# Value blocks in pairs of 512 columns, pass-one tiles and tables in the second weight slot, block 2's rounding copies behind the last h

## The chip, the cores and the metric

One core of a Trainium2 chip. The metric is the device time of one execution in microseconds (us). The kernel before took 1279.45 us, the median of three runs (1277.96 to 1279.61).

## What is computed

One layer of a bidirectional encoder trunk, for one sequence of 2048 tokens of 1024 float32 values. Cut to what matters here:

```python
mod = c_act @ w_ada + b_ada; shift, scale, gate = split(mod, 3)
h = rmsnorm(x, norm_w) * (1 + scale) + shift                  # 2048 x 1024
proj = h @ w_in + b_in                                        # 1024 x 4624
na_q, na_k, na_v, na_z, ml_q, ml_k, ml_v, ml_o, ml_z, gates = split(proj)
na_out = neighbourhood_attention(na_q, na_k, na_v, rpb) * silu(na_z)
mq, mk = split(silu(short_conv(concat(ml_q, ml_k))), 2)
hm = mlstm(mq, mk, ml_v, gates) + flip(mlstm(flip(...)))      # 4 heads of 128, chunks of 64 tokens
ml_out = norm(hm * sigmoid(ml_o)) * ml_norm_w * silu(ml_z)
y = concat(na_out, ml_out) @ w_out;  out = rmsnorm(x + gate * y, final_norm_w)
```

The change is in the input projection `h @ w_in`, above all in the columns ml_v and ml_o (packed by head: a block holds v and o of one head) and na_v, and in places that later stages borrow.

## The kernel before, in words

**Products.** Every float32 operand of a large product is split in a high and a low part, and a product is three matmuls for each of KT = 8 slices of 128 of the contraction (mm3, L636): high by high, high by low, low by high. h lies with its channels on the partitions, as hhi and hlo, in NG = 4 groups of 512 tokens (GT); a group has four token tiles of 128.

**Blocks.** The columns of w_in come in blocks of 256. Blocks 0 to 3 are v and o of the four mLSTM heads (vo_group, L700), block 0 with 16 gate columns more; 4 and 5 are na_v (nav_group, L667). Their result has tokens on the partitions: one token tile is 24 matmuls of 256 columns into one PSUM buffer of the pool `pp` (four buffers), which DVE evicts with one addition of the bias row `brow` (L711, L674). A group of vo gets a sigmoid on ACT (L717) and goes to memory (`d_ck`). Blocks 6 to 9 are computed the other way round, 512 tokens per matmul (`pc`, conv_blocks). Later stages compute the rest (`pq`, L1094) between steps of the mLSTM, where they are pumped in as cover.

**Weights.** There are two slots, `whi_a`/`wlo_a` and `whi_b`/`wlo_b`, used in turn. raw_w (L197) loads a block in two halves of four slices, each half into its one buffer `raw0` or `raw1`; ACT copies it, rounded, into the high part (L207), and DVE subtracts for the low part (L208). SP issues the loads in program order, and each issue waits for whatever it needs: the buffer, and the transfer that stood eight earlier on its lane (names DMAHW0 to DMAHW7).

**The start** (start, L213 to L573) is written out by hand. It computes mod on DVE, h of group 0 slice by slice (first_h, L404: two ACT passes, `hhi` and `h`; DVE makes hlo, L405) and the products of blocks 0 and 1 with each slice k (products, L436). Block 2's group 0 (a third weight place, `w_extra`, borrowed from a later h) follows; its halves are rounded on ACT by high_w2 (L445) at k = 5 and 6, ahead of that slice's products and behind its h, and subtracted on DVE by low_w2 (L449). Then come groups 1 to 3 of blocks 0 and 1, with h of the next group made in between.

**The token blocks** (tok_blocks, L776): block 2's groups 1 to 3, then blocks 3, 4 and 5, each with all four groups, one slot after the other. While a block runs, the next one's halves are loaded at its beginning and split after its groups 1 and 2. One step of a chain of small work is taken after every eviction: gate rows and their two transposes on TensorE (L813), absolute value, exponential and logarithm (L827, L828), scans, decays, gate sums (`gsum`, with loads `ga`), and the column sums `ps_cols` on TensorE (L877). SP also issues nine fills of attention tables (`d_t`, L759) and the preparation of their bias (`d_e`, `rneg`).

**Later places.** Pass one of the mLSTM (ml_pass1) reads tiles `kv` (seven buffers) and weighs them for the two directions. Pass two writes its result in place into `zt` (end, L1405), from which it is stored to `d_mix`. The attention stage keeps four tables `tab` and a ring of ten buffers, four of which are the places of hm and zt.

## Time and profile before

| | |
|---|---|
| median of three runs | 1279.45 us |
| profiled execution | 1278.1 us |
| its span | 1276.3 us |
| granted TensorE clock, mean | 0.997 of full speed |
| TensorE (PE) busy | 1265.2 us, 99% of the span |
| VectorE (DVE) busy | 791.9 us, 62% |
| ScalarE (ACT) busy | 539.3 us, 42% |
| GpSimd (POOL) busy | 201.4 us, 16% |

The span is the time from the first to the last instruction of the profiled execution. A group's "mean ns" is the length of one instruction; matmuls overlap, so what one of them costs is read from the distance of two starts. In a row of the timeline stand its start, its length, the engine, the line, the operation and, in square brackets, how long the engine had been idle before it and what ended that. PEclk in a window is the clock that TensorE was granted, as a share of full speed.

### The profile page before, as it was taken

To read this page: it belongs to the slowest core of one execution; us is meant where nothing else is said; L and a number is where in the kernel's file an instruction comes from. 1 tells how busy PE (TensorE), PEld (TensorE's weight loads), DVE (VectorE), ACT (ScalarE), POOL (GpSimd) and SP (SyncE) were. 2 spreads that over 40 slices of the span, in tenths; PEclk is the share of its full clock that TensorE was granted. 3 is DMA by queue.
4 is the path that set the end of the run, shared out by engine and by line. 5 is a ranking of instruction groups with operands and counts; after the bars stand their busy time and mean duration, and the time that the engine had idled before them with its cause. 6 is when DMAs were issued, how large, how long until landed. Compare 5 with 4: busy or idle time off the path is not lost.

```text
span 1276.3 us, 22945 instructions
## 1 busy us (share of the span) xinstructions
PE 1265.2 (99%) x8168; PEld 1096.9 (86%) x8168; DVE 791.9 (62%) x2391; ACT 539.3 (42%) x1183; POOL 201.4 (16%) x368
## 2 busy tenths in 40 slices
PE   9999999999999999999999999999999999999997
PEld 8999999999888888888888888888877888888886
DVE  7766542213667665266777878877557766767664
ACT  6652425442333222123333324323357565565552
POOL 0000003341000000000001001001324431332541
PEclk9999999999999999999999999999999999999999
DMA  9999937987678754745757867746678755655551
GB/s 366 333 308 281 305 123 200 238 228 199 188 173 200 167 147 109 212 126 168 201 170 204 243 195 218 233 156 180 208 251 265 229 163 161 203 176 178 173 175 67
DMA packets 217082, 259.08 MB, mean 203 GB/s; under 512 B 23435, under 2 KB 163595, under 8 KB 216968
## 3 DMA queue, kind: packets, MB, share of 16 engines
q1 hardware_dynamic: 149542, 190.09, 51.7%
q0 software_dynamic: 13616, 37.28, 9.0%
q10 hardware_dynamic: 53810, 30.24, 8.4%
q8 instruction: 65, 1.06, 0.3%
q14 instruction: 49, 0.40, 0.1%
HBM read 173.05 MB, written 92.72 MB: 208 GB/s over the span
## 4 chain that ended last, share of the span: by engine, by line
PE 94%; DMA 4%; DVE 1%; issue 1%; ACT 0%; SPq 0%; POOL 0%; ACTq 0%; POOLq 0%
PE pq L1094 27%; PE y L1676 14%; PE pc L640 5%; PE pc L641 5%; PE pc L639 5%; PE pO L1633 4%; PE pT L1618 3%; PE pvo L639 3%; PE pvo L641 3%; PE pvo L640 3%; PE pS L1587 3%; PE pvo L694 3%; PE pv L641 2%; PE pv L640 2%; PE pv L639 2%; PE pi L1346 2%
## 5 line engine op out<-in xcount | busy, mean ns | idle before, releaser
L1094 PE MATMUL pq<-hhi,whi_a 128*128 128x512 f32 x512 | 208.4, 407 | 0.0
L1094 PE MATMUL pq<-hlo,whi_a 128*128 128x512 f32 x512 | 207.9, 406 | 0.0
L1094 PE MATMUL pq<-hhi,wlo_a 128*128 128x512 f32 x512 | 207.2, 405 | 0.0
L1368 POOL TENSOR_TENSOR hm<-hm,ck 128x128 f32<-128x128 f32 x64 | 28.3, 442 | 576.3 <-DVE hm L1367 541.5
L1094 PEld LDWEIGHTS pq<-hhi,wlo_a 128*128 128x128 f32 x512 | 96.8, 189 | 16.6 <-issue 0.2
L1094 PEld LDWEIGHTS pq<-hlo,whi_a 128*128 128x128 f32 x512 | 96.8, 189 | 16.1 <-issue 0.4
L1094 PEld LDWEIGHTS pq<-hhi,whi_a 128*128 128x128 f32 x512 | 96.8, 189 | 16.0
L1599 ACT ACTIVATE ring<-ring,mn 128x480 f32<-128x480 f32 (+5 forms) x128 | 75.9, 594 | 55.8 <-DVE mn L1598 55.8
L1620 ACT ACTIVATE ring<-pT 96x384 f32<-96x384 f32 (+3 forms) x128 | 65.8, 514 | 63.3 <-PE pT L1618 61.8
L1676 PE MATMUL y<-hhi,wlo_a 128*128 128x512 f32 (+1 forms) x272 | 87.0, 394 | 0.2 <-ACT y L1683 0.2
L1676 PE MATMUL y<-hhi,whi_a 128*128 128x512 f32 x256 | 86.3, 408 | 0.0
L1349 ACT ACTIVATE num<-px,gtile 128x129 f32<-128x129 f32 x120 | 38.7, 367 | 105.4 <-PE px L1344 91.7
L1522 POOL DMA_DIRECT2D v<-d_vna x158 | 79.1, 507 | 15.2 <-DMA xr<-in_x_p_dram 4.5
L1618 PEld LDWEIGHTS pT<-ident,ring 128*128 128x128 f32 (+2 forms) x416 | 51.0, 136 | 19.1 <-ACT ring L1620 3.8
L1618 PE MATMUL pT<-ident,ring 128*128 128x128 f32 (+2 forms) x416 | 66.2, 272 | 0.0
L639 PE MATMUL pvo<-whi_b,hhi 128*128 128x256 f32 x224 | 63.7, 284 | 0.0
L1598 DVE CUSTOM_DVE_ANT_0 ring<-pS,tab 128x480 f32<-128x480 f32 (+5 forms) x128 | 62.1, 540 | 2.6 <-PE pS L1587 2.3
L641 PE MATMUL pvo<-whi_b,hlo 128*128 128x256 f32 x224 | 63.2, 282 | 0.0
L640 PE MATMUL pvo<-wlo_b,hhi 128*128 128x256 f32 x224 | 63.0, 281 | 0.0
L934 ACT ACTIVATE dec<-dec,gtile 128x128 f32<-128x128 f32 x128 | 41.4, 391 | 50.6 <-POOL dec L927 45.9
L711 DVE TENSOR_TENSOR stvo<-pvo,brow 128x256 f32<-128x256 f32 x60 | 24.9, 421 | 53.2 <-PE pvo L641 41.3
L674 DVE TENSOR_TENSOR stv<-pv,brow 128x256 f32<-128x256 f32 x32 | 13.5, 425 | 71.5 <-PE pv L641 65.5
(357 smaller groups left out, 3338.3 us busy)
## 6 DMA issues: line engine op xcount, KB each, us to landing
ck<-d_ck SPq DMA_DIRECT2D x64, 384.5 KB, 3.5
rawq<-in_w_main_dram SPq DMA_DIRECT2D x28, 512.0 KB, 5.1
raw<-in_w_main_dram SPq DMA_DIRECT2D x18, 512.0 KB, 6.2
kv<-d_ck SPq DMA_DIRECT2D x64, 128.5 KB, 3.2
dec<-d_mneg SPq DMA_DIRECT2D x32, 256.0 KB, 6.4
d_ck<-dec ACTq DMA_DIRECT2D x32, 256.0 KB, 7.8
qs<-d_qna SPq DMA_DIRECT2D x30, 256.0 KB, 3.9
xr<-in_x_p_dram POOLq DMA_DIRECT2D x15, 512.0 KB, 4.0
```

The lines of the kernel that those rows point to most:

```text
L639: nc.tensor.matmul(ps, lhi(k), rhi(k), start=(k == 0), stop=False)
L640: nc.tensor.matmul(ps, lhi(k), rlo(k), start=False, stop=False)
L641: self.mark = nc.tensor.matmul(ps, llo(k), rhi(k), start=False, stop=(k == KT - 1))
L934: nc.scalar.activation(t[:, o, :], t[:, o, :], AF.Exp, bias=self.cols["g"][:, d, h, c : c + 1])
L1094: self.mark = nc.tensor.matmul(patch_ps(ps) if patch else ps, w, self.htok(h, g, k, patch), start=(k == 0 and n == 0), stop=(k == KT - 1 a ...
L1522: queue.dma_start(chunks[key][r * nkc : (r + 1) * nkc, :], rows[r])
L1598: nc.vector.tensor_tensor_reduce(pt[:, :nk], ps, tabs[ct][:, j * nk : (j + 1) * nk], 1.0, 3e38, ALU.add, ALU.min, mn)
L1599: nc.scalar.activation(pt[:, :nk], pt[:, :nk], AF.Exp, bias=mn, scale=-1.0, accum_out=sums[:, j : j + 1])
L1618: nc.tensor.transpose(ps[:cs, i, :], U[u][j][:, i * cs : (i + 1) * cs], self.ident)
L1620: nc.scalar.activation(t[:cs, :nch, :], ps[:cs, :nch, :], AF.Copy)
L1633: nc.tensor.matmul(po[j * HD : (j + 1) * HD, ct, :], v[:n, h * HD : (h + 1) * HD], pt[j][:n, i, :], start=(i == 0), stop=(i == nch - 1))
L1676: nc.tensor.matmul(y, m[:, k, :], w[k][:, cs], start=(k == 4 and n == 0), stop=(k == 3 and n == 2))
```

## The change

- The two weight slots become one tile per part with a leading index of two (`wpair`), so that slots 0 and 1 lie side by side; both stay for the whole program.
- tok_blocks runs (block, group) in the order (2,1), (3,0), 2 and 3 together for groups 2 and 3, (3,1), (4,0), 4 and 5 together for groups 1 to 3, (5,0). "Together" is pair_group: one matmul of 512 columns reads 256 columns of either slot, and DVE evicts the two halves with one addition each. There are two more staging buffers.
- The halves of block 3 are loaded as soon as block 2's are split, at the end of the start (next_w), and split during (2,1); block 4's during (3,1), block 5's during (4,0), block 6's during (5,0).
- In the start, high_w2 moves from k = 5 and 6 to k = 6 and 7.
- The two gate transposes write one PSUM tile, one behind the other.
- Pass one's tiles lie in slot 1's high part and zt in its low part; both directions' weighted tiles are new tiles (eight buffers); end writes to hm, from which it is stored. Tables lie in slot 1 (the last of the first four loaded behind close); the ring has two places of hm and eight of its own.

The core of the diff:

```diff
-        for nm, pl in (("a", wa), ("b", wb)):
-            self.wslot.append(tuple(pl.tile([P, KT, 272 if nm == "a" else 256], F32R, name=f"w{part}_{nm}") for part in ("hi", "lo")))
+        self.wpair = tuple(wa.tile([P, 2, KT, 272], F32R, name=f"w{part}") for part in ("hi", "lo"))
+        self.wslot = [tuple(part[:, j] for part in self.wpair) for j in range(2)]
...
-            if k in (KT - 3, KT - 2):
-                high_w2(k - KT + 3)
-            if k == KT - 2:
-                low_w2(0)
+            if k in (KT - 2, KT - 1):
+                high_w2(k - KT + 2)
             if k == KT - 1:
                 for tt in range(4, 8):
                     square(tt, ssqs[1])
+                low_w2(0)
                 low()
                 low_w2(1)
...
         def next_w():
-            for part in self.raw_w(2, 0):
+            self.parts = []
+            for half, part in enumerate(self.raw_w(2, 0)):
                 yield
                 part(nc.vector)
+                self.parts.append(self.raw_part(3, 1, half))
...
+    def pair_group(self, blk, g):
...
+        for o in range(4):
+            ps = self.pp.tile([P, GT], F32, tag="pp", name=f"p2_{blk}_{g}_{o}")
+            self.mm3(
+                ps.rearrange("p (a c) -> p a c", a=2),
+                lambda k: self.hhi[g][:, k, o * P : (o + 1) * P],
+                lambda k: self.hlo[g][:, k, o * P : (o + 1) * P],
+                lambda k: hi[:, :, k, :256],
+                lambda k: lo[:, :, k, :256],
+            )
+            for j, st in enumerate(sts):
+                row, part = self.brows[(blk + j) % 2], ps[:, 256 * j : 256 * j + 256]
...
+                next(self.chain, None)
+            next(self.mid, None)
...
     def tok_blocks(self, chain_pool):
...
+        order = [(2, 1), (3, 0), (2, 2), (2, 3), (3, 1), (4, 0), (4, 1), (4, 2), (4, 3), (5, 0)]
+        both = ((2, 2), (2, 3), (4, 1), (4, 2), (4, 3))
+        self.load_bias(3)
+
+        def splits(rest, after):
+            for _ in range(rest):
+                yield
+            for part in self.parts:
+                part(self.nc.vector)
+                yield
+            if after:
+                self.parts = self.raw_w(*after)
...
+        turns = {0: (1, (4, 0)), 4: (0, (5, 1)), 5: (0, (6, 0)), 9: (0, None)}
...
-            t = tiles[k] = ml.tile([P, 257], F32, tag="kv", bufs=7, name=f"kv_{h}_{order[k]}")
+            t = tiles[k] = self.spare(0, k % 7 * 257, 257)
...
-            nc.vector.scalar_tensor_tensor(z, ps, self.mlw[:, h : h + 1], z, ALU.mult, ALU.mult)
-            src = zt[gi]
+            src = hm[gi]
+            nc.vector.scalar_tensor_tensor(src.rearrange("p a q -> p (a q)"), ps, self.mlw[:, h : h + 1], z, ALU.mult, ALU.mult)
```

How the instructions stand now is shown at two places. The first is ACT in the start, from the last rounding copies of blocks 0 and 1 (wr) on. `w_extra<-raw_2_0` is block 2's first rounding copy, `hhi0<-tp_0_6` is h of slice 6. Before:

```order
L314 ACTIVATE whi_b_124<-wr_1_3_289 128x512
L445 ACTIVATE w_extra_154<-raw_2_0_346 128x1024
L404 ACTIVATE hhi0_102<-tp_0_6_498,shT_98,gT_97 128x512
L404 ACTIVATE h_0_6_545<-tp_0_6_498,shT_98,gT_97 128x512
L445 ACTIVATE w_extra_154<-raw_2_1_467 128x1024
L404 ACTIVATE hhi0_102<-tp_0_7_540,shT_98,gT_97 128x512
```

And ACT at the same place after the change:

```order
L312 ACTIVATE whi_119<-wr_1_3_284 128x2x256
L402 ACTIVATE hhi0_102<-tp_0_6_493,shT_98,gT_97 128x512
L402 ACTIVATE h_0_6_539<-tp_0_6_493,shT_98,gT_97 128x512
L443 ACTIVATE w_extra_149<-raw_2_0_341 128x1024
L402 ACTIVATE hhi0_102<-tp_0_7_534,shT_98,gT_97 128x512
L402 ACTIVATE h_0_7_572<-tp_0_7_534,shT_98,gT_97 128x512
L443 ACTIVATE w_extra_149<-raw_2_1_462 128x1024
```

Each rounding copy has moved behind the two passes of a slice's h. The order of the subtractions on DVE is the same.

The second place is the end of the start and the beginning of tok_blocks. SP's issues before, from block 2's bias (`brow0`) to the first gate weights (`ga`); `d_t12` and `d_t22` are table fills, `raw_2_0` is half 0 of block 2:

```order
L682 DMA brow0_129<-in_b_row_dram 128x256 [waits DMAHW0_49,DVE_49]
L203 DMA raw_2_0_1560<-in_w_main_dram 128x1024 [waits DMAHW1_49]
L203 DMA raw_2_1_1562<-in_w_main_dram 128x1024 [waits DMAHW2_49]
L722 DMA d_ck_61<-stvo_0_3_1520 128x4x257 [waits DMAHW3_49,Activation_49,Pool_49]
L759 DMA d_t12_80<-big_132 2048x1x180 [waits DMAHW4_49]
L759 DMA d_t22_83<-big_132 2048x1x144 [waits DMAHW5_49]
L722 DMA d_ck_61<-stvo_1_3_1532 128x4x257 [waits DMAHW6_49,Activation_49,Pool_49]
L597 DMA ga_0_0_1670<-in_w_gt_dram 128x512 [waits DMAHW7_49]
```

SP's issues after, from the same bias to the same store of block 1:

```order
L724 DMA brow0_124<-in_b_row_dram 128x256 [waits DMAHW6_49,DVE_49]
L203 DMA raw_2_0_1555<-in_w_main_dram 128x1024 [waits DMAHW7_49]
L203 DMA raw_2_1_1557<-in_w_main_dram 128x1024 [waits DMAHW0_49]
L587 DMA cact2_1666<-in_small_dram 128x8 [waits DMAHW1_49,PE_49,Activation_49]
L590 DMA d_fnw_69<-in_fnw_dram 16x64 [waits DMAHW2_49]
L596 DMA ga_0_0_1672<-in_w_gt_dram 128x512 [waits DMAHW3_49]
L203 DMA raw_3_0_1587<-in_w_main_dram 128x1024 [waits DMAHW7_49,DMAHW4_49,DVE_49]
L721 DMA d_ck_61<-stvo_0_3_1515 128x4x257 [waits DMAHW5_49,Pool_49]
L203 DMA raw_3_1_1618<-in_w_main_dram 128x1024 [waits DMAHW6_49,DMAHW0_49,DVE_49]
L796 DMA d_t12_80<-big_127 2048x1x180
L796 DMA d_t22_83<-big_127 2048x1x144
L721 DMA d_ck_61<-stvo_1_3_1527 128x4x257 [waits DMAHW1_49,Activation_49,Pool_49]
```

Block 3's halves now stand here, each with a wait on DVE, and the two fills and the store stand behind them; before, block 3's loads came after the gate weights and the `d_e` fills. Block 3's bias stands behind all of these in both kernels.

ACT at that place before, from block 2's copies on; `wide` is the gate rows (exponential, then logarithm):

```order
L207 ACTIVATE whi_a_122<-raw_2_0_1560 128x4x256 [waits DMAHW1_49,PE_49]
L207 ACTIVATE whi_a_122<-raw_2_1_1562 128x4x256 [waits DMAHW2_49,PE_49]
L717 ACT_TABLE_LOAD [waits DMAHW4_49,DVE_49]
L717 ACTIVATE stvo_1_3_1532<-stvo_1_3_1532 128x4x128 [waits Pool_49]
L827 ACT_TABLE_LOAD
L827 ACTIVATE wide_1663<-wide_1663 128x128 [waits DVE_49]
L828 ACT_TABLE_LOAD
L828 ACTIVATE wide_1663<-wide_1663 128x128 [waits Activation_49]
```

ACT after:

```order
L207 ACTIVATE whi_119<-raw_2_1_1557 128x4x256 [waits DMAHW0_49,PE_49]
L588 ACT_TABLE_LOAD [waits DMAHW2_49,DMAHW3_49,DMAHW1_49]
L588 ACTIVATE cact2_1666<-cact2_1666 128x8 [waits Activation_49]
L207 ACTIVATE whi_119<-raw_3_0_1587 128x4x256 [waits DMAHW4_49,PE_49]
L713 ACT_TABLE_LOAD [waits DVE_49]
L713 ACTIVATE stvo_1_3_1527<-stvo_1_3_1527 128x4x128 [waits Pool_49]
L207 ACTIVATE whi_119<-raw_3_1_1618 128x4x256 [waits DMAHW6_49,PE_49]
L880 ACT_TABLE_LOAD
L880 ACTIVATE wide_1665<-wide_1665 128x128 [waits DVE_49]
L881 ACT_TABLE_LOAD
L881 ACTIVATE wide_1665<-wide_1665 128x128 [waits Activation_49]
```

Both copies of block 3 now stand ahead of the gate rows' exponential and logarithm. On DVE, block 3's two subtractions stand behind L883, which uses that logarithm, the second of them behind the scans as well.

More of the change, by code (lines that the diff above doesn't have):

```diff
@@ L170, in phase1 @@
         self.sp = self.pool(ps1a, "sp", bufs=1, space=PSUM)
-        self.tok_blocks(self.pool(toks, "chain", bufs=1, side="right"))
+        chain_pool = self.pool(toks, "chain", bufs=1, side="right")
+        held, more = self.stages, self.pool(toks, "stage2", bufs=2, side="right")
+        self.stages = [*held, more, more]
+        self.tok_blocks(chain_pool)
+        self.stages = held
         toks.close()
@@ L189, in stage_tile, with raw_w, raw_part @@
     def stage_tile(self, name):
-        self.stages.reverse()
-        return self.stages[1].tile([P, 1032], F32, tag="st", name=name).rearrange("p (o c) -> p o c", o=4)
-    def load_w(self, blk, slot, halves=(0, 1)):
-        for part in self.raw_w(blk, slot, halves):
-            part()
-    def raw_w(self, blk, slot, halves=(0, 1)):
+        self.stages.append(self.stages.pop(0))
+        return self.stages[-1].tile([P, 1032], F32, tag="st", name=name).rearrange("p (o c) -> p o c", o=4)
+    def raw_w(self, blk, slot):
+        return [self.raw_part(blk, slot, half) for half in range(2)]
+    def raw_part(self, blk, slot, half):
         nc = self.nc
         hi, lo = self.wslot[slot]
-        def part(half):
+        if True:
             raw = self.raw.tile([P, 4, 256], F32, tag=f"raw{half}", name=f"raw_{blk}_{half}")
@@ L212, in part @@
             return run
-        return [part(half) for half in halves]
     def start(self, left):
@@ L821, in gate_chain @@
         i_r, f_r = new("i_r"), new("f_r")
-        nc.vector.tensor_copy(i_r, transposed(gi, "gi"))
-        nc.vector.tensor_copy(f_r, transposed(gf, "gf"))
+        for row, part in zip((i_r, f_r), transposed((gi, gf))):
+            nc.vector.tensor_copy(row, part)
         yield
@@ L1198, in phase1b, with spare @@
         self.stacks = [pps, right, left]
+    def spare(self, half, start, n):
+        return self.wslot[1][half].rearrange("p a b -> p (a b)").bitcast(F32)[:, start : start + n]
     def close(self):
@@ L1551, in load_x @@
             L[b]["row"] = x
-        tabs = [p.tile([P, 960], F32, name=f"tab{i}") for i in range(4)]
+        tabs = [self.spare(half, start, 960) for half, start in ((0, 0), (0, 960), (1, 1024), (1, 0))]
         def load_tab(b, ct, queue=nc.sync):
```

99 lines of the change are left out of this document (60 added, 39 removed).

## The prediction

> **What bounds the kernel now.** I read the page first, then TensorE's waits over the whole program, then timelines of two places. The page's busy line and chain, and two rows of the waits view:
>
> ```profile
> PE 1265.2 (99%) x8168; PEld 1096.9 (86%) x8168; DVE 791.9 (62%) x2391; ACT 539.3 (42%) x1183; POOL 201.4 (16%) x368
> PE 94%; DMA 4%; DVE 1%; issue 1%; ACT 0%; SPq 0%; POOL 0%; ACTq 0%; POOLq 0%
> ...
> PE pvo L436 <- ACT hhi L404: 2.3, 2, 1.9
> PE dense L348 <- DVE eps L116: 1.1, 1, 1.1
> ```
>
> TensorE (PE) works 99% of the span, and its one wait over 1.1 us is 1.9 us at L436, in the start. So time can come from three things only: fewer nanoseconds per column, that one wait, or new waits. The rest is judged by whether TensorE comes to wait for it. The profiled run took 1278.1 us (span 1276.3 and 1.8 around it), 1.35 under the median of 1279.45; I make the sum as a difference and apply it to the median. A change of 0.2%, 2.56 us, is about what a measurement of this kernel can tell from none.
>
> **Pairs.** TensorE's timeline has the first matmuls of blocks 4 and 5 (256 columns), and two matmuls of the channel blocks (512 columns). Columns: start, duration, engine, line.
>
> ```profile
> 216.81 0.28 PE L639 MATMUL pv<-whi_a,hhi 128*128 128x256 f32 x1
> ...
> 262.25 0.28 PE L639 MATMUL pv<-whi_b,hhi 128*128 128x256 f32 x1
> 337.22 0.40 PE L639 MATMUL pc<-hhi,whi_a 128*128 128x512 f32 x1
> ...
> 341.85 0.40 PE L641 MATMUL pc<-hhi,wlo_a 128*128 128x512 f32 x1
> ```
>
> Durations overlap, so I use starts. A block is 16 tiles of 24 matmuls: 45.44 us over 384 is 118.3 ns each. The two lower rows are 20 matmuls apart: 4.63/20 = 231.5 ns. Two of 256 cost 236.6 ns, so a paired one saves 5.1 ns. Five pair groups of 4 tiles of 24 matmuls are 480: **-2.4 us**, on the path, since TensorE never waits there. The same columns are evicted in the same number of DVE additions. The Trainium skill (TensorE: Matmul & The Clock Gate, "Back-to-back issue gap") gives an isolated matmul N/2.4 + 2.5 ns, so pairing would save 2.5 ns each, an estimate of 1.2 us; these rows say twice that.
>
> **The start.** Timeline of the three engines around k = 6, and the granted clock by microsecond (its columns: stretch, length, busy of PE, PEld, DVE, ACT, POOL, then PEclk):
>
> ```profile
> 35.94 1.28 DVE L259 CUSTOM_DVE_ANT_0 junkv<-mod_hi,c_all,small 128x1024 bf16<-128x1024 f32 x1
> 37.15 0.09 DVE L259 DVE_READ_ACCUMULATOR2_ANT shT<- 128x1 f32 x1
> ...
> 40.83 0.69 DVE L405 TENSOR_TENSOR hlo<-h,hhi 128x512 fp32r<-128x512 f32 x1 [1.13 <-ACT h L404]
> 41.44 1.28 DVE L259 CUSTOM_DVE_ANT_0 junkv<-mod_lo,c_all,small 128x1024 bf16<-128x1024 f32 x1
> ...
> 38.41 1.06 ACT L445 ACTIVATE w_extra<-raw 128x1024 fp32r<-128x1024 f32 x1 [2.06 <-DMA raw<-in_w_main_dram]
> 39.37 0.76 ACT L404 ACTIVATE hhi<-tp,shT,gT 128x512 fp32r<-128x512 f32 x1
> ...
> 42.83 0.78 ACT L404 ACTIVATE hhi<-tp,shT,gT 128x512 fp32r<-128x512 f32 x1 [1.07 <-DVE shT L259]
> ...
> 37.70 0.60 PE L397 MATMUL tp<-ident,x 128*128 128x128 f32 x4
> 40.18 0.40 PE L436 MATMUL pvo<-whi_a,hhi 128*128 128x272 f32 x1 [1.89 <-ACT hhi L404]
> ...
> 47.68 0.28 PE L639 MATMUL pvo<-w_extra,hhi 128*128 128x256 f32 x1
> ...
> 40.00:41.00 1.00, 0.82 (x5) 0.82 (x6) 0.17 (x1) 1.00 (x3) 0.00 (x0) 0.82 1.01 401
> 41.00:42.00 1.00, 1.00 (x6) 1.00 (x6) 1.00 (x2) 0.75 (x1) 0.00 (x0) 0.50 1.06 422
> ...
> 43.00:44.00 1.00, 1.00 (x7) 1.00 (x6) 0.87 (x1) 1.00 (x2) 0.00 (x0) 0.50 1.01 401
> ```
>
> ACT sits at block 2's rounding copy until its weights land at 38.41, and h of k = 6 waits behind it until 39.37, though DVE had its shift at 37.24. TensorE then stands 1.89 us, and its clock reads 0.50 to about 44. With the copy behind h, h6 can start at 37.3 and TensorE at 38.3, right behind its transposes: 1.9 us sooner. What is late next is DVE's shift of k = 7: 41.44 moves up by the 1.13 us that DVE no longer waits for h6, so h7 starts near 41.8 (before 42.83). TensorE's 24 products of k = 6, at about 0.12 us, end near 41.3, and it idles about 1.2 us until h7 is there. 24 more products at full clock end at about 45.6, so the third block's first product, at 47.68 before, comes at about 45.8: **-1.9 us**. If the clock still halves after that pause, the same three microseconds at half speed cost 1.5 again, and only 0.4 is left. The two copies now lie in ACT's idle time ahead of h7 and behind it, and their subtractions keep their place on DVE. I take 1.9, since 1.2 us is well under 1.89.
>
> **Gate transposes.** They now run one behind the other and DVE copies both: at most **-0.1 us**.
>
> **Block 3's weights.** This is the new wait. Before, block 3 was needed 35 us after the start of block 2's remainder; now its group 0 stands right behind (2,1). Its two raw halves use block 2's buffers, so SP loads each one only when DVE has made block 2's low part of that half. Rows of SP, ACT, DVE and TensorE, then the landing times of all raw loads and block 2's first product:
>
> ```profile
> 122.20 0.91 SPq L203 DMA_DIRECT2D raw<-in_w_main_dram  x2
> ...
> 128.75 1.06 ACT L207 ACTIVATE whi_a<-raw 128x1024 fp32r<-128x1024 f32 x1 [2.56 <-DMA raw<-in_w_main_dram]
> 130.08 1.06 ACT L207 ACTIVATE whi_a<-raw 128x1024 fp32r<-128x1024 f32 x1 [0.27 <-DMA raw<-in_w_main_dram]
> ...
> 137.50 1.28 ACT L828 ACT_TABLE_LOAD   x1
> 138.79 0.31 ACT L828 ACTIVATE wide<-wide 128x128 f32<-128x128 f32 x1
> ...
> 131.32 1.21 DVE L208 TENSOR_TENSOR wlo_a<-raw,whi_a 128x1024 fp32r<-128x1024 f32 x1
> ...
> 139.13 0.29 DVE L830 SCALAR_TENSOR_TENSOR wide<-wide 128x128 f32<-128x128 f32 x1 [0.19 <-ACT wide L828]
> 139.46 0.42 DVE L837 TENSOR_TENSOR_SCAN wide<-ones,wide 64x128 f32<-64x128 f32 x1
> ...
> 144.39 0.42 DVE L838 TENSOR_TENSOR_SCAN wide<-ones,wide 64x128 f32<-64x128 f32 x1
> ...
> 146.29 0.13 DVE L848 COPY ends<-wide 64x1 f32<-64x1 f32 x1
> ...
> 132.39 0.28 PE L639 MATMUL pvo<-whi_a,hhi 128*128 128x256 f32 x1
> ...
> DMA to landing us min/median/max: 4.4/6.7/8.8
> ```
>
> All moves up 1.9 us with the start. TensorE begins (2,1) at 130.5 and ends it 96 x 0.1183 us and two transposes later, at 141.9. Block 2's halves land at 126.8 and 128.2; with copy and subtraction (second subtraction now 131.32 to 132.53) SP issues block 3's second half at about 130.7. Let it land L later. ACT rounds it by 130.7 + L + 1.1. Only behind that copy stand the gate chain's exponential and logarithm, two table loads of 1.28 and two of 0.31, 3.2 us; DVE waits for them at L883 (0.3) and only then makes low part 0 (1.2), seven scans and copies (144.39 to 146.42 less a 0.4 sum that lay between, plus the 0.42 scan of 139.46: 2.0), an eviction (0.4) and low part 1 (1.2). So low part 0 is there at 136.5 + L, part 1 at 140.1 + L. TensorE wants part 0 at 141.9 and, 12 matmuls later, part 1. The stall is L - 3.2 us in all: 1.2 at the shortest landing (4.4), 3.5 at the median, 5.6 at the longest. These halves are issued one by one and ahead of the table fills, so I take 5.6 between shortest and median: **+2.4 us**, of which about 2.2 in one piece.
>
> Such a pause is a little over the 1.89 us after which the clock read 0.50, which would cost 1.5 us; there, though, the pause followed 0.6 us of transposes. I count half: **+0.75**. The Trainium skill (same page, "What's actually happening") puts the halving after an idle window of about 3.4 us; by it nothing is added here. The 1.89 us pause speaks against that; I keep the half from the row.
>
> **What queues behind.** SP runs in order. The two last fills and block 3's bias now stand behind block 3's loads and are waited for by lane. Rows: landings of fills and biases, ACT's decay, TensorE's use of it.
>
> ```profile
> d_t<-big SPq DMA_DIRECT2D x2, 1152.0 KB, 17.3
> ...
> brow<-in_b_row_dram SPq DMA_DIRECT2D x6, 128.0 KB, 6.8
> d_mix<-zt ACTq DMA_DIRECT2D x15, 256.0 KB, 4.0
> 157.00 0.31 ACT L874 ACTIVATE dec<-dec 1x128 f32<-1x128 f32 x1 [3.13 <-DVE dec L873]
> 161.81 0.38 PE L877 MATMUL ps_cols<-ones,wide 1*128 1x1 f32 x2
> ```
>
> Fills issued near 131.5 land by 148.8, the bias behind them by 155.8. DVE's evictions of (3,0), and everything queued behind them on DVE, wait for it; four PSUM buffers let TensorE go on until about 156.2, where the first pair needs the first buffer. Of the decay's 4.5 us of slack one or two remain. **+0.3**, bounds 0 and 2.
>
> **Nothing, by cover.** The mLSTM's output is now written into hm, so a new hm waits for a store of 4.0 us twice per head; query products are pumped there, and I cost it at 0 (bound 2). Pass-one tiles in slot 1, eight weighted tiles and ring and table places change addresses, not work; tables that load later are covered by the closing steps.
>
> **Sum.** -2.4 - 1.9 - 0.1 + 2.4 + 0.75 + 0.3 = -0.95. On the median: 1278.5 us.
>
> **The rivals.**
>
> *The loads land early (0.33).* With 4.4 us the stall is 1.2, too short for the clock, and the bias comes in time: -4.4 + 1.2 = -3.2, 1276.3 us; with no stall at all 1275.1. For it: nothing big is in flight when the second half is issued. Against it: block 2's own halves took 6.5 us and more. It is faster from a landing of about 5.0.
>
> *The split becomes the bound (0.21).* Block 3's half lands 8.8 us after its issue, in one queue with checkpoint stores and gate weights; ACT then holds the gate chain behind the copy, DVE the low parts behind the gate chain. TensorE stands 5.6 us, its clock halves (1.5), the bias adds 0.3: -4.4 + 7.4 = +3.0, 1282.4 us. It is slower by more than 0.2% from a landing of 8.4 us, or from 6.9 if the start's clock still halves. For it: 8.8 occurred in this kernel. Against it: the median is 6.7.
>
> *Pairs pay half (0.06).* If the pair's two-piece weight read holds the pitch at 234, pairing gives 1.2 us: 1279.7, no change. The skill's gap of 2.5 ns says this size; the 512-column rows say otherwise, though none of them reads two pieces.
>
> **How the numbers follow.** Forecast 0.40, early loads 0.33, late split 0.21, half pay 0.06. Forecast and half pay are within 0.2%: 0.46. Early loads are faster: 0.33. The late split is slower: 0.21. The forecast's own range, with L from 5.0 to 6.9 and the clock halved or not, is 1277 to 1281. With the other cases it is 1275.1 to 1282.4.
>
> **What the profile after would show.** Right: no wait for hhi at k = 6, one of about 1.2 us at k = 7 with the clock near full; pair matmuls 231 ns apart; a TensorE wait for block 3's low part at the start of (3,0), about 142 us, and half of it gone or doubled with the landing of its raw half. Wrong: no TensorE wait there at all, a wait inside the pair groups, waits for hm in the mLSTM, or a pitch over 234 ns.

## The result and the profile after

The changed kernel takes 1285.74 us (median of 4 runs, 1284.61 to 1286.76) beside 1278.70 us of the kernel before (4 runs, 1276.93 to 1279.61). The ratio is 1.0061, with an interval of 1.0048 to 1.0073: it is slower by 0.6%. The forecast was 1278.5, and no rival ended so high. The profiled execution took 1284.61 us, its span is 1282.5; before it was 1278.1 and 1276.3.

The page of the profile after, busy time and chain:

```profile
PE 1263.4 (99%) x7688; PEld 1071.7 (84%) x7688; DVE 788.4 (61%) x2391; ACT 539.9 (42%) x1183; POOL 200.4 (16%) x368
...
PE 85%; DVE 2%; ACT 1%; issue 0%; DMA 0%; ACTq 0%; DVEq 0%
```

TensorE has 480 matmuls fewer, as the pairs should make it, and is busy 1.8 us less. But VectorE's and ScalarE's shares of the chain are now 2% and 1% (before 1% and 0%). TensorE's waits after (total, times, longest); left out are two in the first steps of the start and small ones:

```profile
PE ht L1454 <- ACT hm L1447: 5.6, 2, 4.8
PE pvo L639 <- DVE ends L900: 2.1, 1, 2.1
PE pvo L434 <- ACT hhi L402: 1.2, 2, 0.8
...
PE pvo L639 <- DVE wlo L208: 0.7, 1, 0.7
```

The 1.9 us wait of the start is gone, block 3's weights are waited for as foreseen, and a new wait of 4.8 us stands at the first row.

To see what each stage got, I take the starts of first products from TensorE's timeline and subtract (`px` is the first product of pass two of a head of the mLSTM). In us:

| from, to | before | after | difference |
|---|---|---|---|
| span's start to block 2's first product (start) | 47.68 | 46.02 | -1.66 |
| to the first pc (blocks 2 to 5, pairs among them) | 260.13 | 260.76 | +0.63 |
| to the first pq (channel blocks, convolution) | 185.45 | 185.02 | -0.43 |
| to the first px (head 0) | 69.70 | 69.70 | 0 |
| to the last head's first px (called heads 0 to 2 below) | 279.06 | 280.25 | +1.19 |
| to the span's end (head 3, close, attention, output) | 434.27 | 440.71 | +6.44 |

The sum is 6.2 us. The last row alone is the loss. (The 0.43 us that the convolution gained were not forecast, and were not looked into.) I use the same stretches below, and not medians alone, since the start has a spread of its own: in 10 of the 14 profiled executions the granted clock reads 0.50 for 6.8 or 10.2 us somewhere between 9.8 and 20.3 us, in kernels that do the same work up to there, before and after not among them.

**Where the loss is.** VectorE's, GpSimd's, ScalarE's and TensorE's timeline after, at the end of head 3, where the last rows of hm are normalized: var, a reciprocal root by integer steps (rstd), mu, then ACT's scaling and TensorE's transposes.

```profile
907.49 0.17 DVE L1432 TENSOR_SCALAR var<-mv 128x4 f32<-128x4 f32 x1
907.70 4.81 DVE L1497 TENSOR_SCALAR rstd<-var 128x4 int32<-128x4 int32 x1
912.54 0.16 DVE L1510 TENSOR_TENSOR nwt<-rstd 128x4 f32<-128x4 f32 x1
...
907.11 1.11 POOL L1558 DMA_DIRECT2D qs<-d_qna  x2 [0.30 <-POOL hm L1422]
908.21 4.27 POOL L1803 MEMSET ring<- 128x512 f32 x9
...
915.61 1.65 ACT L1447 ACTIVATE hm<-hm,mu,rstd 128x128 f32<-128x128 f32 x4 [6.06 <-DVE mu L1435]
...
916.15 0.48 PE L1454 MATMUL ht<-ident,hm 128*128 128x128 f32 x1 [4.80 <-ACT hm L1447]
...
913.00:917.00 4.00, 0.85 (x4) 0.71 (x4) 2.31 (x9) 1.39 (x4) 2.00 (x4) 0.54 0.65 165
917.00:921.00 4.00, 4.00 (x13) 3.17 (x12) 0.00 (x0) 0.49 (x2) 0.00 (x0) 0.61 0.75 235
```

A step on 128x4 numbers takes 4.81 us and ends at 912.51, within 0.03 us of the end of nine memsets of the attention's ring (912.48). Everything behind it comes that much later: mu, ACT's scaling, TensorE's transposes. And the clock is at half from 913.3 to 920.1 us: it reads 0.61 on the average of the 4 us from 917. The same place before:

```profile
907.97 0.25 DVE L1443 TENSOR_SCALAR rstd<-var 128x4 int32<-128x4 int32 x1
908.25 0.16 DVE L1456 TENSOR_TENSOR nwt<-rstd 128x4 f32<-128x4 f32 x1
...
910.88 0.16 DVE L1458 SCALAR_TENSOR_TENSOR rstd<-nwt,rstd 128x4 f32<-128x4 f32 x1
...
907.02 0.53 POOL L1748 MEMSET ring<- 128x512 f32 x1
...
908.24 1.10 POOL L1557 DMA_DIRECT2D tab<-d_t  x2
909.31 0.56 POOL L1504 DMA_DIRECT2D qs<-d_qna  x1
909.83 3.37 POOL L1748 MEMSET ring<- 128x512 f32 x7
```

There the step took 0.25 us, beside the issue of table loads, and the seven memsets came only when VectorE was at the later steps, which are of other forms and ran in 0.16 us beside them. So the change's places did move something in time: with the tables in slot 1 GpSimd issues its two table loads earlier (at 832 and 836 us, before at 908), nothing stands any more between the qs loads and the memsets, and nine of the ring's buffers (its eight own and one place of hm) are cleared in one run, just when the step comes.

**What came as foreseen.** TensorE's timeline after: the start's last wait and block 2's first product; the two waits at (3,0); the first pair matmul of block 4 and the product that follows the last one of three pair groups. Then ACT and VectorE at (3,0).

```profile
42.57 0.39 PE L434 MATMUL pvo<-whi,hhi 128*128 128x272 f32 x1 [0.83 <-ACT hhi L402]
...
46.02 0.28 PE L638 MATMUL pvo<-w_extra,hhi 128*128 128x256 f32 x1
...
143.13 0.39 PE L639 MATMUL pvo<-wlo,hhi 128*128 128x256 f32 x1 [0.74 <-DVE wlo L208]
...
146.95 0.38 PE L639 MATMUL pvo<-wlo,hhi 128*128 128x256 f32 x1 [2.15 <-DVE ends L900]
147.18 0.28 PE L640 MATMUL pvo<-whi,hlo 128*128 128x256 f32 x1
...
228.69 0.40 PE L638 MATMUL p<-whi,hhi 128*128 128x512 f32 x1
...
295.44 0.28 PE L638 MATMUL pv<-whi,hhi 128*128 128x256 f32 x1
...
134.41 1.06 ACT L207 ACTIVATE whi<-raw 128x1024 fp32r<-128x1024 f32 x1 [3.44 <-DMA raw<-in_w_main_dram]
...
136.78 0.64 ACT L713 ACTIVATE stvo<-stvo 128x512 f32<-128x512 f32 x1
137.33 1.04 ACT L207 ACTIVATE whi<-raw 128x1024 fp32r<-128x1024 f32 x1
...
141.65 0.29 DVE L883 SCALAR_TENSOR_TENSOR wide<-wide 128x128 f32<-128x128 f32 x1 [4.40 <-ACT wide L881]
141.86 1.22 DVE L208 TENSOR_TENSOR wlo<-raw,whi 128x1024 fp32r<-128x1024 f32 x1
...
145.69 1.21 DVE L208 TENSOR_TENSOR wlo<-raw,whi 128x1024 fp32r<-128x1024 f32 x1
```

The clock at this place after, by microsecond (clock in the last column but two):

```profile
146.00:147.00 1.00, 0.05 (x1) 0.05 (x1) 0.97 (x3) 0.00 (x0) 0.00 (x0) 1.00 1.13 277
147.00:148.00 1.00, 1.00 (x8) 1.00 (x9) 0.96 (x3) 0.34 (x1) 0.00 (x0) 1.00 1.06 324
```

The pair pitch (the distance of two starts) is 66.75 us over 288 matmuls, 231.8 ns. At (3,0) the order of events is the predicted one: ACT's second copy, the two table loads and activations, L883, low part 0, the scans, low part 1.

### The profile page after: what moved, and what is told of

The parts are those of the page before. It is cut to its first block, busy times and chain, and to the rows that moved or that the text cites. A ratio compares the mean times of both kernels' runs of the same rounds, so it can differ in the third digit from the quotient of the medians.

```text
span 1282.5 us, 22069 instructions
## 1 busy us (share of the span) xinstructions
PE 1263.4 (99%) x7688; PEld 1071.7 (84%) x7688; DVE 788.4 (61%) x2391; ACT 539.9 (42%) x1183; POOL 200.4 (16%) x368
## 4 chain that ended last, share of the span: by engine, by line
PE 85%; DVE 2%; ACT 1%; issue 0%; DMA 0%; ACTq 0%; DVEq 0%
PE pq L1147 27%; PE y L1730 14%; PE pc L639 5%; PE pc L638 5%; PE pc L640 5%; PE pO L1687 4%; PE pT L1672 3%; PE p L639 3%; PE p L638 3%; PE p L640 3%; PE pS L1641 3%; PE pi L1400 2%; PE px L1398 2%; PE dc L1337 2%; PE a L1385 1%; PE pv L640 1%
## 5 line engine op out<-in xcount | busy, mean ns | idle before, releaser
L1147 PE MATMUL pq<-hhi,whi 128*128 128x512 f32 x512 | 208.9, 408 | 0.0
L1147 PE MATMUL pq<-hlo,whi 128*128 128x512 f32 x512 | 208.8, 408 | 0.0
L1147 PE MATMUL pq<-hhi,wlo 128*128 128x512 f32 x512 | 208.0, 406 | 0.0
L1147 PEld LDWEIGHTS pq<-hhi,whi 128*128 128x128 f32 x512 | 97.2, 190 | 16.5
L1147 PEld LDWEIGHTS pq<-hhi,wlo 128*128 128x128 f32 x512 | 97.3, 190 | 16.4 <-issue 0.2
L1147 PEld LDWEIGHTS pq<-hlo,whi 128*128 128x128 f32 x512 | 97.1, 190 | 16.2 <-issue 0.4
L638 PE MATMUL pc<-hhi,whi 128*128 128x512 f32 x256 | 101.8, 398 | 0.0
L639 PE MATMUL pc<-hlo,whi 128*128 128x512 f32 x256 | 101.5, 397 | 0.0
L640 PE MATMUL pc<-hhi,wlo 128*128 128x512 f32 x256 | 100.5, 393 | 0.0
L1730 PE MATMUL y<-hhi,wlo 128*128 128x512 f32 (+1 forms) x272 | 86.9, 394 | 0.2 <-ACT y L1737 0.2
```

Source lines behind the costliest of these rows:

```text
L638: nc.tensor.matmul(ps, lhi(k), rhi(k), start=(k == 0), stop=False)
L639: nc.tensor.matmul(ps, lhi(k), rlo(k), start=False, stop=False)
L640: self.mark = nc.tensor.matmul(ps, llo(k), rhi(k), start=False, stop=(k == KT - 1))
L1147: self.mark = nc.tensor.matmul(patch_ps(ps) if patch else ps, w, self.htok(h, g, k, patch), start=(k == 0 and n == 0), stop=(k == KT - 1 a ...
L1730: nc.tensor.matmul(y, m[:, k, :], w[k][:, cs], start=(k == 4 and n == 0), stop=(k == 3 and n == 2))
```

## The experiments

All change the kernel after, except the one that says otherwise. The kernel before was run beside each. "Stretch" is a row of the table above.

**The memsets behind the step (e1).**

```diff
+                self.last_mu = mu
...
+        first = nc.gpsimd.tensor_copy(few.tile([P, 4], F32, name="after_mu"), self.last_mu)
         for t in ring[2:] + ring[:2]:
-            nc.gpsimd.memset(t, 0.0)
+            self.behind(nc.gpsimd.memset(t, 0.0), first)
```

A small copy on GpSimd reads mu, and the memsets are ordered behind it.

> The changed kernel, with GpSimd's memsets of the ring put behind its loads and behind a small copy that waits for the last group's mu. Theory: VectorE's small TENSOR_SCALAR (the first step of the last rstd, 4.81 us instead of 0.17) is held as long as GpSimd runs its nine memsets in one piece; with them behind it, it takes about 0.2 us, TensorE's 4.8 us wait ahead of ht and the half clock behind it (1.4 us) go, and the time is 1279.5 us (6.2 less). Rival 1: it is GpSimd's issuing of transfers that holds the step; here six are issued in a row from about 907 to 911 us, so the step still takes about 3.5 us and the time is about 1284. Rival 2: the step waits for something that has nothing to do with GpSimd; then nothing changes, 1285.7.

1282.59 us (7 runs), ratio to before 1.0034 (1.0022 to 1.0046). Its rows of VectorE and GpSimd:

```profile
912.04 0.17 DVE L1498 TENSOR_SCALAR rstd<-var 128x4 int32<-128x4 int32 x1
...
911.44 1.11 POOL L1559 DMA_DIRECT2D qs<-d_qna  x2 [0.30 <-POOL hm L1422]
912.54 2.01 POOL L1574 DMA_DIRECT2D v<-d_vna  x3
...
915.29 0.18 POOL L1803 COPY after_mu<-mu 128x4 f32<-128x4 f32 x1
915.41 4.26 POOL L1805 MEMSET ring<- 128x512 f32 x9
```

The step takes 0.17 us while GpSimd issues DMAs all around it, so issuing is not what held it. The last stretch is 434.44, beside 434.27 of before: 6.27 of the 6.44 us are the memsets. The time came down by only 3.15 us, where 6.2 were expected. Block 2's first product stands at 50.28 us here, 4.3 later than in the trace after, with the clock at half from 10 to 20 us; and all seven runs have a mean clock of 0.993 to 0.996, where 8 of the 12 of before beside them have 0.999. The start is the same work in both, so I read the stretches; what they still lose is the subject of e6 and e7.

**Six of the nine in front (e2).** The copy of mu without the order behind it; the program then puts six memsets in front of the copy and three behind.

```diff
-            self.behind(nc.gpsimd.memset(t, 0.0), first)
+            nc.gpsimd.memset(t, 0.0)
```

> The changed kernel, with only six of the nine memsets in one piece and then a small copy on GpSimd that waits for the last mu, which stands behind the held step. Theory: the step ends with the sixth memset, 908.2 + 6 x 0.53 = 911.4 us, 1.1 us sooner than before (3.7 us long), TensorE's wait shrinks from 4.8 to 3.7 and the time to about 1284.6. Rival 1 (issuing of transfers) and rival 2 (something else): the step ends at 912.5 as before, 1285.7.

1285.59 us (4 runs), ratio 1.0057 (1.0042 to 1.0072); last stretch 439.09. The median can't tell the 1284.6 of the theory from the 1285.7 of the rivals; the rows can:

```profile
911.10 3.41 DVE L1498 TENSOR_SCALAR rstd<-var 128x4 int32<-128x4 int32 x1
...
911.61 2.88 POOL L1805 MEMSET ring<- 128x512 f32 x6
```

The step ends at 914.51, the sixth memset at 914.49, though three more memsets follow later.

**Seventeen memsets (e3).** All but two ring buffers are cleared twice.

```diff
             nc.gpsimd.memset(t, 0.0)
+            if t is not ring[0] and t is not ring[1]:
+                nc.gpsimd.memset(t, 0.0)
```

> The changed kernel, with each of eight ring places set to zero twice, 17 memsets in one piece instead of nine. Theory: the step is held to about 908.2 + 17 x 0.53 = 917.2 us, 4.3 us longer than before (9.1 us), and the time is about 1290. Both rivals: no change of the step, 1285.7.

1290.74 us (4 runs), ratio 1.0100 (1.0086 to 1.0114); last stretch 445.67. Rows of VectorE, of GpSimd (the last memset) and of TensorE's waits:

```profile
910.34 8.56 DVE L1497 TENSOR_SCALAR rstd<-var 128x4 int32<-128x4 int32 x1
...
918.32 0.55 POOL L1803 MEMSET ring<- 128x512 f32 x1
...
PE ht L1454 <- ACT hm L1447: 9.4, 2, 8.5
```

The step ends at 918.90, the last memset at 918.87. With 6, 9 and 17 memsets it takes 3.41, 4.81 and 8.56 us, and the last stretch grows by 4.6, 6.3 and 11.2 us over e1's: the hold and about a third on top, which is the halved clock behind the pause.

**Another form of the step (e4).** The same arithmetic, with the constant in a tile, so that the instruction is a SCALAR_TENSOR_TENSOR; the memsets stay where they are.

```diff
+        self.magic = c.tile([P, 4], mybir.dt.int32, name="magic")
+        nc.vector.memset(self.magic, 0x5F3759DF)
...
-        nc.vector.tensor_scalar(y.bitcast(I32), v.bitcast(I32), -0.5, 0x5F3759DF, ALU.mult, ALU.add)
+        if n == 1:
+            nc.vector.tensor_scalar(y.bitcast(I32), v.bitcast(I32), -0.5, 0x5F3759DF, ALU.mult, ALU.add)
+        else:
+            nc.vector.scalar_tensor_tensor(y.bitcast(I32), v.bitcast(I32), -0.5, self.magic[:, :n], ALU.mult, ALU.add)
```

> The changed kernel with its memsets as they are; the first step of the rstd of four columns is done as a SCALAR_TENSOR_TENSOR with a small tile of constants in place of the TENSOR_SCALAR with a constant. Theory: it is the form of the step that is held (scalar_tensor_tensor and tensor_tensor steps ran at their usual 0.16 us beside seven memsets in the kernel before); it takes about 0.2 us here, and the time is 1279.5. If any step at that place is held by the memsets: 4.8 us again in whichever step stands there, 1285.7. Rival 2: the step's successor or itself still ends at 912.5, 1285.7.

1283.16 us (6 runs), ratio 1.0040 (1.0025 to 1.0055); last stretch 436.39.

```profile
911.35 0.16 DVE L1502 SCALAR_TENSOR_TENSOR rstd<-var,magic 128x4 int32<-128x4 int32 x1
914.37 0.16 DVE L1437 SCALAR_TENSOR_TENSOR mu<-mv,rstd 128x4 f32<-128x4 f32 x1
...
911.86 4.28 POOL L1808 MEMSET ring<- 128x512 f32 x9
```

The step starts as far ahead of the memsets' row as the held ones did (0.5 us) and takes 0.16 us; the chain up to mu then runs beside the memsets. So it is the form of the instruction. The last stretch is 1.9 us longer than e1's, with no wait of TensorE to show for it. Set product beside product, the difference grows evenly over the whole stretch: 0.25 us before the memsets begin, 0.29 behind the close, 1.85 at the end; and the row of head 0, which ends long before, is 69.88 beside 69.69 or 69.70 in all others. So it isn't the memsets, nor the loads of v that stand behind them here: this execution ran a little slower all along, and why stays open.

**The start alone (e5).** The kernel before, with nothing changed but the place of block 2's rounding copies.

```diff
-            if k in (KT - 3, KT - 2):
-                high_w2(k - KT + 3)
-            if k == KT - 2:
-                low_w2(0)
+            if k in (KT - 2, KT - 1):
+                high_w2(k - KT + 2)
...
+                low_w2(0)
```

> The kernel before with only the start's part of the change: block 2's rounding copies behind h of k = 6 and 7. Theory: the third block's first product comes at about 46.0 us as in the changed kernel, against 47.68 in the profiled run before, in which the clock had halved after the 1.89 us pause; where it does not halve there, the gain is the smaller idle time alone. Time 0.5 to 1.7 us less: 1276.3 us beside 1277.3 for the kernel before. Rival: the pause at k = 7 (0.8 to 1.2 us) halves the clock instead, no gain, 1277.3.

1276.96 us (11 runs) beside 1277.70 (30 runs): 0.9998 (0.9989 to 1.0007). No gain can be measured, and at most 1.4 us of the predicted 1.9 fit into the interval. The profiled execution had its clock at half from 11 to 18 us and reached block 2 at 48.45, so its trace doesn't size the term.

**Block 3 without the gate chain (e6).** e1, and the chain of gate rows starts only with (3,0).

```diff
+            if n == 0:
+                held, self.chain = self.chain, iter(())
+            if n == 1:
+                self.chain = held
```

> The changed kernel with the memsets behind (as in e1) and with the gate chain held back until (3,0), so that ScalarE's exponential and logarithm and VectorE's scans no longer stand between block 3's rounding and its low parts. Theory: block 3's second low part ends about 1.3 us after its rounding copy, near 140 us, ahead of TensorE; the two waits at (3,0) (0.9 and 2.3 us between starts) go, and from the third block's first product to the first product of block 6 it takes 257.5 us instead of 260.6. Time about 1279.4 against 1282.6 for e1. Rival: the bias and table loads queued behind on SP, or the later chain, become the next wait; then the stretch shrinks by less than 1.5 us.

1281.41 us (11 runs), ratio 1.0024 (1.0014 to 1.0035). Both waits at (3,0) are gone, but others stand in their place; TensorE's waits:

```profile
PE p L638 <- DVE stvo L753: 1.6, 1, 1.6
...
PE kt L1102 <- ACT acc_k L1093: 0.9, 1, 0.9
```

The first is a pair group waiting for the evictions of (3,0), which wait for block 3's bias; the second comes in the convolution. The stretch of blocks 2 to 5 is 259.50 (e1 260.62), that of the convolution 186.16 (185.02): what the first gains the second gives back, and the 3 us that were expected are not there.

**Three buffers for hm (e7).** e1, and hm has three buffers (the ring then takes three of its places from hm and seven of its own).

```diff
-                hm[gi] = self.mle.tile([P, 4, CH], F32, tag="hm", bufs=2, name=f"hm_{h}_{gi}")
+                hm[gi] = self.mle.tile([P, 4, CH], F32, tag="hm", bufs=3, name=f"hm_{h}_{gi}")
```

> The changed kernel with the memsets behind (as in e1) and three buffers for hm instead of two (the ring takes three places of hm and seven of its own), so that a new hm no longer waits for the store of the one two groups back. Theory: VectorE's eight waits for d_mix stores (7.9 us in all) go, and with them what the mLSTM lost: from the first px of head 0 to that of head 2 it takes 185.9 us as before the change instead of 187.4; time about 1281.2 against 1282.6 for e1. Rival: the loss comes from pass one's order (both directions weighed into new tiles, the wait of 0.8 to 1.0 us at ht at the head's end); then that stretch stays at 187 us or more.

1279.75 us (11 runs), ratio 1.0015 (1.0006 to 1.0024). VectorE's waits after the change had this row, in which a new hm waits for the store of the old one:

```profile
DVE hm L1420 <- DMA d_mix<-hm: 7.9, 8, 1.4
```

It is not in e7's waits. Heads 0 to 2 take 279.09 us, beside 280.25 after, 280.44 in e1 and 279.06 before: the stores cost 1.2 to 1.4 us, and this edit takes all of it back. The other traces agree: with two buffers 279.92 to 281.62 us in six, with three 278.76 to 279.09 in six.

**e6 and e7 together (e8)**, one diff on top of the other.

> The changed kernel with the memsets behind, the chain held back and three buffers for hm. Theory: the three savings add: 1285.7 - 4.8 to 6.4 - 3.1 - 1.4, that is 1275 to 1278 us by how the clock falls in the start, against 1277.3 for the kernel before. Rival: one of them gives its saving back as another wait; then over 1279.

1281.38 us (8 runs), ratio 1.0027 (1.0016 to 1.0037). Blocks 2 to 5 take 257.80 us, 2.3 under before, and heads and close are back. But the convolution takes 188.84 (185.45 before):

```profile
PE kt L1102 <- ACT acc_k L1093: 3.0, 3, 1.6
```

The held chain ends later: ScalarE's last decays run until 306.9 us (in e7 until 300.5). But that they cause these waits is not shown. ScalarE had stood for 9 us ahead of its activations of acc_k at 352.54 and 379.18 and waited for VectorE, whose steps for acc_k stand behind steps that wait for loads of w_out (23.0 us between 306 and 380 us, 19.1 in e7).

**A mend that failed (e9).** e8, with block 3's bias loaded ahead of the fills and two chain steps per eviction in (4,0).

```diff
+            if (blk, g) == (4, 0):
+                next(self.chain, None)
...
+        self.load_bias(3)
         ...
-        self.load_bias(3)
```

> The kernel of e8 (memsets behind, chain held back to (3,0), three buffers for hm) with two more edits: block 3's bias is loaded ahead of the relative-bias loads and the d_e fills, and the gate chain takes two steps at each eviction of (4,0), so that the four steps held back are made up. Theory: the bias lands by 150 us, ahead of its first eviction, and the decays no longer reach into block 6; from the third block's first product to the first product of block 6 it takes 257.5 us, block 6 to the first query product 185.0 (e8: 188.8). Time about 1275.5 where the start's clock holds, 1277 to 1279 as a median. Rival: the conv stage's waits for ScalarE come from something else than the chain, and stay: 188 and 1281.

1282.46 us (7 runs), ratio 1.0032 (1.0021 to 1.0043). The convolution's stretch stays at 188.70, by another wait, with the clock at half behind it:

```profile
PE pc L638 <- ACT whi L207: 2.4, 1, 2.4
```

Block 6's copies (307.52, after the change 300.83, of which 2.7 us are the later start) stood behind the decays, of which the last ended at 307.1.

**Pairs as halves (e10).** e7, and each paired matmul of 512 columns is issued as two of 256 into the same bank.

```diff
-            self.mm3(
-                ps.rearrange("p (a c) -> p a c", a=2),
...
+            for j in range(2):
+                self.tok_tile(ps[:, 256 * j : 256 * j + 256], self.wslot[(blk + j) % 2], 4 * g + o)
```

> The kernel of e7 (memsets behind, three buffers for hm) with each pair matmul of 512 columns issued as two of 256, in the same order of groups. Theory: 480 x 5 ns = 2.2 to 2.4 us more between the third block's first product and that of block 6 (260.0 to 262.3), time about 1282 beside 1279.75 for e7. Rival by the 2.5 ns of the page's gap: 1.2 us more. Rival: the longer groups give VectorE and SP more room, and nothing is lost.

1281.01 us (10 runs), ratio 1.0025 (1.0016 to 1.0034). Blocks 2 to 5 take 262.57 us beside 260.02 in e7: pairing is worth 2.55 us, 5.3 ns for each of 480.

**Block 3's bias first (e11).** e7, and its load is issued ahead of the tables' fills.

```diff
+        self.load_bias(3)
         ...
-        self.load_bias(3)
```

> The kernel of e7 with block 3's bias loaded ahead of the relative-bias loads and the d_e fills, the chain as in the changed kernel. Theory: TensorE does not wait for the bias there (four buffers cover it), so the two waits at (3,0) stay at 0.6 to 0.9 and 2.2 us and the stretch at 260 us; time as e7, 1279.75. Rival: the late bias holds VectorE's chain and with it ps_ends and ps_cols; then the stretch shrinks by 0.5 us or more.

1280.34 us (11 runs), ratio 1.0019 (1.0010 to 1.0028). The stretch is 260.33 beside 260.02: with the gate chain in its place the late bias costs nothing. It was late only in e6, where (3,0) came sooner.

**Block 3 one group later (e12).** e7, and (2,2) stands between (2,1) and (3,0); four pair groups are left of five.

```diff
-        order = [(2, 1), (3, 0), (2, 2), (2, 3), (3, 1), (4, 0), (4, 1), (4, 2), (4, 3), (5, 0)]
-        both = ((2, 2), (2, 3), (4, 1), (4, 2), (4, 3))
+        order = [(2, 1), (2, 2), (3, 0), (2, 3), (3, 1), (3, 2), (4, 0), (4, 1), (4, 2), (4, 3), (5, 0)]
+        both = ((2, 3), (4, 1), (4, 2), (4, 3))
...
-        turns = {0: (1, (4, 0)), 4: (0, (5, 1)), 5: (0, (6, 0)), 9: (0, None)}
+        turns = {0: (1, (4, 0)), 4: (0, (5, 1)), 6: (0, (6, 0)), 10: (0, None)}
```

> The kernel of e7 (memsets behind, three buffers for hm) with one pair group less: the order is (2,1), (2,2), (3,0), 2 and 3 together for group 3, (3,1), (3,2), (4,0), 4 and 5 together for groups 1 to 3, (5,0). Block 3's split has 11.4 us more before its first product, and the gate chain keeps its place. Theory: no wait at (3,0), one pair group (0.47 us) less of gain: 258.1 us from the third block's first product to that of block 6 where e7 has 260.0 and the kernel before 260.1; block 6 to the first query product stays at 185.0. The two things together give 1.9 us less than e7, about 1277.5 as a median and 1275.3 where the start's clock holds, that is 0 to 2 us under the kernel before. Rival: as in e8 and e9 something behind gives it back (block 6's weights, the bias at (3,0)): 260 or 188 us in these stretches, 1280.

1277.18 us (11 runs, 1275.55 to 1278.93) beside 1278.26 (15 runs): 0.9991 (0.9982 to 1.0000). Its ratio is the lowest of all versions; it is 1 us under the kernel before, at the edge of what can be told. TensorE's longest waits:

```profile
PE pvo L434 <- ACT hhi L402: 1.2, 2, 0.8
PE c L350 <- ACT c_all L344: 1.2, 1, 1.2
PE dense L346 <- DVE eps L116: 1.1, 1, 1.1
```

All three are in the start; none is left at (3,0), in the heads or at the close. Blocks 2 to 5 take 257.79 us, the convolution 185.04. From block 2's first product to the end it takes 1226.55 us of a span of 1275.2, the kernel before 1228.62: the gain is 2.1 us, of which this execution lost 1.0 again in the start, where its clock was at half from 11 to 18 us.

## Why the prediction was wrong

Against its own execution the sum was -0.95, and +6.5 was measured.

**The step that failed** is "Pass-one tiles in slot 1, eight weighted tiles and ring and table places change addresses, not work; tables that load later are covered by the closing steps". Places decide what waits for what, and so when GpSimd's memsets run; I costed the queue by its addresses and never asked which engine works beside it. The memsets came to lie on VectorE's first rstd step. Shown by moving them behind (e1, -6.3 us in the last stretch), by fewer and by more of them (e2, e3), and by another form of the step (e4): the hold of 4.81 us, 4.6 more than before, stands on the path, for nothing of TensorE's work is left to cover the last transposes. The pause of 4.80 us also halves the clock: eight products 0.43 us apart (0.23 at full speed) are another 1.6 us. The table loads that I looked at were indeed covered. The Trainium skill (SBUF — State Buffer, "Who interferes with whom") has the rule that I should have weighed: VectorE and GpSimd share a pair of ports, tensor_scalar can be in a mode that takes it, and then whichever came second "fully blocks" until the other's instruction is done, while an instruction with two SBUF inputs is disturbed only by a GpSimd instruction that reads. The rows agree on which form is held: the TENSOR_SCALAR is, the SCALAR_TENSOR_TENSOR beside memsets is not. They add that one hold lasts over memsets that follow each other: the step waited for the last of 6, 9 and 17. They don't agree on the order: by its record the held step started 0.51 or 0.52 us ahead of the first memset in all three, where by that rule the memset would have been second, and 0.17 us are all that the step needs in e1. Whether the record of a memset begins late isn't known. That it is the ports is the Trainium skill's explanation; no run here looks at them.

**Waits for hm.** "I cost it at 0 (bound 2)": it was 1.2 to 1.4 us (e7). The mechanism was named, the value was wrong: the query products didn't cover it, since it is VectorE that stands, eight times, and TensorE's transposes follow it.

**Block 3's weights.** Right in mechanism, size off: 2.4 was forecast, 3.2 was lost (the two starts come 0.9 and 2.3 us later than the pitch would have them). My L was the landing of the second half, taken as 5.6: issued at 130.88, it landed 6.15 us later, at 137.04, and that is 0.55 of the 0.8. The rest is ACT's queue: the copy started only at 137.33, without a wait on DMA, since ACT had the activation of a checkpoint in front of it, with a table load of its own from 135.49. Together it is as if L were 6.4.

**The half clock behind that pause.** 0.75 was counted, 0 came: the clock read 1.00 all along, and the products behind the 2.15 us wait are 0.12 us apart again from the second on. The idle window of about 3.4 us of the Trainium skill (TensorE: Matmul & The Clock Gate, "What's actually happening"), which I set aside for the row of before, fits here and at the close (4.80 us, halved); read as a pause of that length, it doesn't fit the 1.89 us in the start of before, nor the 2.38 us in e9, which was followed by half clock too. What differs between the short pauses is in the traces. In each of the fourteen, all changes of the clock lie whole multiples of 3.41 us apart. I cut the traces at these points into stretches of 3.41 us. From 25 us on, a stretch in which TensorE stood for 1.89 us or more in all was each time followed by half clock (1.89 before, 1.95 after, 2.02 in e9), and one with 1.73 us or less never was. The 2.15 us pause fell across such a point, 0.52 us ahead of it and 1.63 behind; in the eight executions that have this pause, no stretch holds more than 1.73. So what I lacked is where a pause lies between these points, which its length alone doesn't tell.

**Pairs.** 2.4 forecast; 2.2 by the pitches (118.2 and 231.8 ns in the trace after, 480 times 4.6), 2.2 to 2.55 by e10 against e11 and e7. Right, and the two-piece weight read costs nothing, so the rival "pairs pay half" falls.

**The start.** -1.9 forecast, -1.66 between the two traces, and nothing measurable by e5. k = 6 no longer waits, and k = 7 waits 0.83 us where 1.2 was worked out. Part of the 1.66 is the half clock in before's trace from 40.65 to 44.06 us. At least 40 of the 79 runs of before beside the experiments lack it: their mean clock is 0.999, so at most 1.9 us of full clock were lost, while the end of the span alone lost 0.95 to 2.4 us in the fourteen traces and 3.41 us at half would add 1.7. Among the runs with 0.999, the four of e5 have a median of 1276.6 us and the twelve of before beside them 1277.19: 0.6 us less, near the 0.4 of my lower case. So the step that failed in this term is that the half clock behind the pause was read from one execution as if all had it.

**The queue behind.** 0.3 forecast, 0 by e11. **The gate transposes** (-0.1) were not tried alone.

**The rivals.** The late split, the one on the slower side, had the landing of 8.8 us as its cause; it didn't happen. Slower came from a mechanism that stood in the list of things costed at nothing.

## What to carry to other kernels

When a change moves buffers, list for each engine what now runs beside what at the places where TensorE's cover ends; a place alone can bring nine memsets forward onto a step that the end waits for. Before a term is set to zero as "only addresses", look at the order of the other engines at the close of a stage, above all GpSimd beside a small TENSOR_SCALAR of VectorE. A small copy that reads the last result, with the clearing ordered behind it, took 6.3 us off the last stretch, all but 0.2 of its loss. And before a pause or a clock of one trace goes into a sum, look at the mean clock of the other runs: it tells whether they have it too.

## What the runs showed of the hardware

- A VectorE TENSOR_SCALAR of 128x4 numbers took 3.41, 4.81 and 8.56 us beside 6, 9 and 17 GpSimd memsets of 128x512 that followed each other without a gap, and 0.17 us beside GpSimd's issue of six DMAs. SCALAR_TENSOR_TENSOR and TENSOR_TENSOR beside memsets took 0.16.
- In the start, with TensorE idle for at most 0.08 us in the 3.41 us ahead, the granted clock fell to 0.50 in 10 of 14 profiled executions, for 6.8 or 10.2 us, which moves block 2's first product from about 46 to 48.5 or 50.3 us. A mean clock of 0.996 or less, at least 4.5 us of full clock lost, stands in 18 of the 79 runs of before beside the experiments, but in 42 of the 69 runs of e1, e6, e7, e8 and e10 to e12, which do the same work in the first 20 us; why is open.
- TensorE's pauses of 1.89, 2.38 and 4.80 us were followed by half clock, eight of 2.15 us were not. The clock changed only at points 3.41 us apart, and a stretch between two of them with 1.89 us or more of idle TensorE was followed by half clock, one with 1.73 or less was not (from 25 us on).
